# Reordered first norm, two more gate buffers, modulation transposes right behind a product, residual additions of the projection on GpSimd

## The chip, the cores and the metric

The kernel runs on one core of a Trainium2 chip. The metric is the device time of one execution in microseconds, as the median of several executions. Each engine has its own stream of instructions and works through it strictly in order; an instruction that waits for something holds up everything behind it on its engine.

## The reference, cut to what matters

The kernel computes one step of a diffusion backbone with one layer. The 128 prompt tokens and 1024 latent tokens are handled together as 9 tiles of 128 tokens, with 1024 features. Prompt and latent tokens have modulation rows of their own.

```
mod  = silu(c) @ w_mod + b_mod                       # shift1, scale1, gate1, shift2, scale2, gate2
h    = rmsnorm(x) * (1 + scale1) + shift1            # the first norm
p, v, g1, g2 = split(h @ w_in)                       # pool input, LRU input, two gates
v    = conv(v);  r, i = sigmoid(v @ w_r + b_r), sigmoid(v @ w_i + b_i)   # per head, two directions
a    = exp(-8 * r * softplus(-lambda));  u = sqrt(1 - a^2) * i * v
y    = scan(a, u) forward + scan(a, u) backward      # final prompt states are an output
m    = sigmoid(g1) * (pool(p) @ w_bp) + sigmoid(g2) * (y @ w_bl)
x    = x + gate1 * (m @ w_out)                       # "the projection"
h2   = rmsnorm(x) * (1 + scale2) + shift2            # the second norm
aff  = softmax(h2 @ router);  16 experts each take their best tokens  # expert-choice MoE
x    = x + gate2 * moe(h2);   y = rmsnorm(x)
```

## The kernel before, in words

The program's order on each engine is the order in which the code issues instructions; nothing reorders them afterwards. Weights arrive in float32 (`raw`, `araw`); a split makes of each piece a rounded high half on ACT (line L188, `hi` or `vh`) and the rest on DVE (L189, `lo` or `vl`), and a product is three products: high by high (L198), low by high (L199), high by low (L200). `do_split(n)` issues the splits up to entry n of a list, and loads run ahead of it.

**First norm (about 28 to 90 us).** The features come in eight column blocks k of 128, handled as four quarters q of two blocks. For each quarter, `mod_first` multiplies the conditioning with pieces of `w_mod` (the first four pieces in float32 at L386, the others split, L389), `mod_low` copies the sums to a small row `mrow`, `mod_second` turns that into columns on PE (L401), and DVE makes `modc` (L405) and `s` (L407) of them. `hn_first` modulates and splits block 2q in three parts (L361, L362 ACT, L365 DVE). `hn_cols` (L354 DVE, L355 ACT) and `hn_low` (L368 DVE) do it for block 2q+1. `dense_v(j, k)` multiplies block k into two accumulators, those of `v` for j = 0 and 1. `softplus` (L126 to L141) stands at the end of this stage.

**Input projection (to about 430 us).** The list `seq` orders products of w_in (`v`, `g2`, `g1`, `p`) and 256-column pieces of the modulation (`m`). Each `v` product is followed by `gates` (sigmoids, L527), `gates_rest` and `scans` of a neighbouring block. Gate tiles and the low half `yl` of a scan's result share five buffers, tag `gate`. A piece of modulation (`mod_block`, L665 and L666) leaves a row `mrow`; its transposes (`mod_cols`, L213) and their DVE part (L217, L218) are put off by five turns of the main loop, in `later`, and run at the head of a turn, ahead of its product. `pool_evac(g)` copies a `p` product to `ppad` (four ACT copies, L613 to L616), calls `pool_mm(g-1)` and then does the windowed sums that end in `ph` (L641) and `plo` (L642). `states` transposes the scans' final states, `st_c` (L692).

**Projection and routing (about 700 to 803 us).** `project(i, h)` makes tile i, half h of m @ w_out: 24 products (L984 to L986), then on DVE `tmp` = product times gate (L980) and the addition to the residual row `x2s[i]` (L981; its buffer is called `sg`, two buffers). Behind both halves come `norm2` (L992, L999, L1000, whose result is stored by SP at L1003), `router_a` (eight transposes at L1015, issued in the middle of the next tile's first half, ACT copies L1016), `router_b` (L1022) and `router_c` (L1026). The rows `x2s[i]` are loaded at L961 on SP, behind the stores of the second norm. When tiles are through, `affinities` (L1036 to L1044), `first_cols` (L1081) and `first_row` (L1092 on PE) prepare the ranks (L1111, L1114). From about 900 us on the experts run.

Of the kernel before, what the change touches and what calls it, by code (L numbers as in the profile page):

```python
# [8 lines left out]
F32 = mybir.dt.float32  # L9
# [18 lines left out]
DP = range(4)  # L28
# [21 lines left out]
def hybrid_step_kernel(ctx: ExitStack, tc: tile.TileContext, x_prompt, x_sample, state_lru, c, c_ctx,  # L50
# [70 lines left out]
    l_a = ini.tile([P, 16], F32, name="l_a")  # L121
    l_e = ini.tile([P, 16], F32, name="l_e")
    l_z = ini.tile([P, 16], F32, name="l_z")
    l_q = ini.tile([P, 16], F32, name="l_q")

    def softplus():  # L126
        A.activation(l_a, lamc, AF.Abs)
# [35 lines left out]
    s1 = const.tile([P, 2, KD], F32, name="s1")  # L163
# [131 lines left out]
    junk = xsp.tile([P, D], F32, name="junk")  # L295
    vsp = [[xsp.tile([P, 1024], F32R, name=f"v{n}{j}") for n in ("h", "l")] for j in range(2)]
# [55 lines left out]
    def hn_cols(k):  # L352
        for x, z in ((xv[:, k, 0, :SP], 0), (xv[:, k, 0, SP:], 1), (xv[:, k, 1:], 1)):
            V.tensor_scalar(x, x, s1[:, z, k:k + 1], modc[:, 0, z, k:k + 1], op0=OP.mult, op1=OP.add)  # L354
        A.copy(hn_hi[:, k, :].rearrange("p (g t) -> p g t", g=3), xv[:, k])  # L355
# [37 lines left out]
    def mod_low(q):  # L393
        mrow1[q] = xsp.tile([P, D], F32, name="mrow1", tag="junk")[:4, :512]
        A.copy(mrow1[q][:, :256], mps[q][:4, :256])
        (A.copy if q else V.tensor_copy)(mrow1[q][:, 256:], mps[q][:4, 256:])
# [32 lines left out]
    do_split(4)  # L429
    norm1(2)  # L430
    x_cols1(1, 0, A)
    x_cols1(1, 1, A)
    mod_first(0)
# [4 lines left out]
    mod_first(3)  # L438
    mod_low(0)
    do_split(5)  # L440
# [3 lines left out]
    hn_first(0)  # L444
    do_split(8)

    for q in range(4):
        k = 2 * q
        if q < 3:
            do_split(4 * q + 10)  # L450
        dense_v(0, k)
        for n in (4, 5) if q < 3 else ():
            mod_first(4 * q + n)
        hn_cols(k + 1)
        dense_v(1, k)
        for n in (6, 7) if q < 3 else ():
            mod_first(4 * q + n)
        hn_low(k + 1)
        if q < 3:
            mod_low(q + 1)  # L460
            do_split(4 * q + 12 if q < 2 else HEAD + 2)
        dense_v(0, k + 1)
        if q < 3:
            mod_second(q + 1)
        dense_v(1, k + 1)
        if q < 3:
            hn_first(k + 2)
    softplus()
# [49 lines left out]
    def gates(j):  # L518
        vc, vhi, vlo, ghi, glo = LR[j]
        gt = []  # L520
        for m in range(4):
# [4 lines left out]
            r = lt.tile([P, LT], F32, name="gate", bufs=5)  # L526
# [24 lines left out]
    def scans(j):  # L551
# [11 lines left out]
        yl = lt.tile([P, T], F32R, name="yl", tag="gate", bufs=5)  # L563
# [45 lines left out]
    def pool_evac(g, a3):  # L609
# [5 lines left out]
        for q in range(2):  # L615
            A.copy(lat[:, 4 + 6 * q:10 + 6 * q], a3[:, 1 + q, :CH].rearrange("p (r c) -> p r c", c=GW))  # L616
        if g:
            pool_mm(g - 1)
# [41 lines left out]
    def mod_block(q, h, w):  # L660
# [6 lines left out]
        if h:  # L667
            mrow = mrp.tile([4, 256], F32, name="mrow", bufs=2)
            A.copy(mrow, t[:4, :256])
            later.append([5, lambda: mod_cols(1 + q // 8, 2 * (q % 8), 2, mrow)])  # L670
# [37 lines left out]
    conv(0)  # L708
    for j in range(2):
# [12 lines left out]
    for i in range(HEAD + 2, len(seq)):  # L722
        kind, j = seq[i]
        if kind == "m" and (kind, j) not in spl and i < done_split[0]:
            continue
        if (kind, j) != ("g1", 0):
            do_split(i + 4)
        for d in list(later):
            d[0] -= 1
            if d[0] <= 0:  # L730
                d[1]()
                later.remove(d)
        if kind == "bl" and j == 0:
# [25 lines left out]
        else:  # L759
            a3 = dense(w, KD, hn_hi, hn_lo)  # L760
        if kind == "g1" and j:
# [4 lines left out]
        if kind == "v":  # L766
            v_evac(a3)
            if seq[i + 1][0] == "m":
                n = seq[i + 1][1]
                mod_block(n // 2, n % 2, spl.pop(("m", n)))  # L770
# [184 lines left out]
    def project(i, h, mid=(), part=False):  # L955
# [25 lines left out]
        V.tensor_tensor(x2s[i][:, hs], x2s[i][:, hs], tmp, op=OP.add)  # L981
# [815 lines left out]
```

## Time and profile before

| what | value |
|---|---|
| median of 3 executions | 2153.65 us (2150.96 to 2155.9) |
| the profiled execution: time, and its span in the trace | 2155.95 us, 2154.2 us |
| PE busy | 2070.4 us, 96% of the span |
| DVE busy | 1709.6 us, 79% |
| ACT busy | 1358.8 us, 63% |
| GpSimd (POOL) busy | 190.9 us, 9% |

The profiled execution is 2.3 us longer than the median; 1.75 us of its time lie outside the span. All places below are microseconds from the start of the span. A busy time in the trace is the time in which an engine executed; what its instruction waited for stands in square brackets, with the idle time before it. PEclk is the granted TensorE clock, 1.0 being 2.4 GHz and 0.5 being 1.2 GHz.

### The profile page before, as it was taken

How to read it: one execution, taken by the hardware profiler on the slowest of the kernel's cores; microseconds unless marked ns; L12 is line 12 of the kernel's file. 1: busy time of each engine (PE TensorE's matmuls, PEld its weight loads, DVE VectorE, ACT ScalarE, POOL GpSimd, SP SyncE). 2: the span in 40 equal slices, each digit the busy share in tenths (PEclk: the TensorE clock that was granted, in tenths of full speed). 3: DMA queues.
4: the chain of work that ended last, by engine and by line, in shares of the span. 5: the costliest groups of instructions: out<-in, count | busy, mean ns of one | idle time of the engine just before them, and what ended most of it. 6: DMA issues, size and time to landing. Idle time of an engine off the chain costs nothing.

```text
span 2154.2 us, 40533 instructions
## 1 busy us (share of the span) xinstructions
PE 2070.4 (96%) x17269; PEld 1974.4 (92%) x17269; DVE 1709.6 (79%) x1847; ACT 1358.8 (63%) x1444; POOL 190.9 (9%) x324
## 2 busy tenths in 40 slices
PE   6999999999999987899999999999999999999995
PEld 4799998999998875899999999999999999999994
DVE  6788988732236467988988898998998998899896
ACT  6477675321112225677877777877877777777783
POOL 0000001010101001020010010011010011011021
PEclk9999999999999988999999999999999999999997
DMA  8133434174644238699999999999999999999995
GB/s 265 56 118 114 125 111 124 55 223 117 203 158 170 109 110 296 237 326 332 346 328 334 343 331 324 343 340 326 333 335 327 338 341 328 336 341 323 339 313 181
DMA packets 304820, 543.91 MB, mean 252 GB/s; under 512 B 16300, under 2 KB 85628, under 8 KB 304639
## 3 DMA queue, kind: packets, MB, share of 16 engines
q1 hardware_dynamic: 285306, 478.56, 64.0%
q0 software_dynamic: 15728, 52.77, 8.4%
q10 hardware_dynamic: 3604, 9.98, 1.4%
q8 instruction: 135, 2.21, 0.4%
q14 instruction: 47, 0.38, 0.1%
HBM read 500.60 MB, written 40.67 MB: 251 GB/s over the span
## 4 chain that ended last, share of the span: by engine, by line
PE 86%; DVE 8%; DMA 2%; ACT 2%; issue 1%; SPq 0%; DVEq 0%; ACTq 0%
PE ac L1465 37%; PE ac L1473 17%; PE a L198 6%; PE a L199 6%; PE a L200 6%; PE a L757 5%; DVE lo L1280 2%; PE a L984 1%; PE a L986 1%; PE a L985 1%; DMA xg<-hn_d,lgi 1%; PE tp L1404 1%; PE tp L1489 1%; DVE lo L189 1%; PE tp L665 1%
## 5 line engine op out<-in xcount | busy, mean ns | idle before, releaser
L1280 DVE TENSOR_TENSOR lo<-raw,hi 128x2048 bf16<-128x2048 f32 x384 | 870.9, 2281 | 0.0
L1274 ACT CAST hi<-raw 128x2048 fp32r<-128x2048 f32 x384 | 729.4, 1912 | 3.8 <-issue 2.2
L1465 PE MATMUL ac<-x,hi 128*128 128x288 f32 x4096 | 606.1, 300 | 0.0
L1465 PEld LDWEIGHTS ac<-x,hi 128*128 128x128 f32 x4096 | 553.0, 189 | 1.0 <-issue 0.9
L1473 PEld LDWEIGHTS <-lo 128*128 128x128 bf16 x6144 | 380.4, 98 | 36.7 <-DVE lo L1280 0.8
L1465 PE MATMUL ac<-hh,hi 128*128 128x288 f32 x2048 | 332.9, 304 | 0.0
L1478 ACT COPY bs<-ac 128x288 f32<-128x288 f32 x320 | 127.8, 399 | 290.6 <-PE ac L1473 289.1
L1473 PE MATMUL ac<-xb,lo 128*128 128x144 bf16 x4096 | 302.4, 227 | 0.6 <-DVE lo L1280 0.6
L1465 PEld LDWEIGHTS ac<-hh,hi 128*128 128x128 f32 x2048 | 279.9, 189 | 0.0
L198 PE MATMUL a<-hn_hi,hi 128*128 128x384 f32 x624 | 212.0, 340 | 0.0
L199 PE MATMUL a<-hn_lo,hi 128*128 128x384 f32 x624 | 210.8, 338 | 0.0
L200 PE MATMUL a<-hn_hi,lo 128*128 128x384 f32 x624 | 210.8, 338 | 0.0
L1473 PE MATMUL ac<-hb,lo 128*128 128x144 bf16 x2048 | 171.9, 227 | 0.0
L189 DVE TENSOR_TENSOR lo<-raw,hi 128x1024 fp32r<-128x1024 f32 (+1 forms) x76 | 86.7, 1163 | 78.8 <-ACT hi L188 78.2
L1479 DVE TENSOR_TENSOR h<-ac,bs 128x288 f32<-128x288 f32 x256 | 115.7, 452 | 42.1 <-ACT bs L1478 41.8
L198 PEld LDWEIGHTS a<-hn_hi,hi 128*128 128x128 f32 x624 | 117.1, 188 | 0.4
L199 PEld LDWEIGHTS a<-hn_lo,hi 128*128 128x128 f32 x624 | 117.2, 188 | 0.0
L200 PEld LDWEIGHTS a<-hn_hi,lo 128*128 128x128 f32 x624 | 117.2, 188 | 0.0
L1710 POOL TENSOR_TENSOR yps<-ot,modc 128x128 f32<-128x128 f32 x16 | 35.9, 2247 | 735.2 <-DVE ot L1479 735.2
L188 ACT CAST hi<-raw 128x1024 fp32r<-128x1024 f32 (+1 forms) x76 | 74.8, 1001 | 41.2 <-PE a L199 33.3
L1479 DVE TENSOR_TENSOR ot<-ac,bs 128x288 f32<-128x288 f32 x64 | 29.3, 457 | 69.7 <-ACT bs L1478 69.7
L699 ACT ACTIVATE sg<-a 128x1152 f32<-128x1152 f32 x16 | 18.1, 1134 | 82.4 <-PE a L200 82.3
(447 smaller groups left out, 2626.8 us busy)
## 6 DMA issues: line engine op xcount, KB each, us to landing
raw<-in_exp_w_dram SPq DMA_DIRECT2D x380, 1024.0 KB, 7.2
raw<-in_w_in_dram SPq DMA_DIRECT2D x28, 512.0 KB, 5.0
raw<-in_w_mod_dram SPq DMA_DIRECT2D x28, 512.0 KB, 5.3
araw<-in_w_mod_dram SPq DMA_DIRECT2D x18, 256.0 KB, 4.5
g_d<-sg ACTq DMA_DIRECT2D x8, 576.0 KB, 3.2
yh_d<-yh POOLq DMA_DIRECT2D x8, 576.0 KB, 3.1
yl_d<-yl POOLq DMA_DIRECT2D x8, 576.0 KB, 4.6
m_d<-sg POOLq DMA_DIRECT2D x8, 576.0 KB, 4.2
```

Source lines behind the costliest of these rows:

```text
L188: A.copy(h, raw)
L189: V.tensor_tensor(l, raw, h.bitcast(F32), op=OP.subtract)
L198: PE.matmul(out, whi, xhi, start=first, stop=False)
L199: PE.matmul(out, whi, xlo, start=False, stop=False)
L200: PE.matmul(out, wlo, xhi, start=False, stop=last)
L757: PE.matmul(a3[:, ch, :CH], w[:, k, :], y[:, k, cs], start=n == 0 and k == 0 and w is hi, stop=n == 1 and k == KD - 1 and w is ws[-1])
L1274: A.copy(hl[n][0], raw[n])
L1280: V.tensor_tensor(lo, r, hi.bitcast(F32), op=OP.subtract)
L1465: PE.matmul(a[:, r, :2 * S], w[0][:, k, c0 + r * P:c0 + (r + 1) * P], x2(kk), start=kk == first, stop=False)
L1473: PE.matmul(a[:, r, S:2 * S], w[1][:, k, c0 + r * P:c0 + (r + 1) * P], xb(kk), start=False, stop=kk == last)
L1478: A.copy(b, a[:, :, S:2 * S])
L1479: V.tensor_tensor(dst, a[:, :, :S], b, op=OP.add)
```

## The change

There are six edits.

1. The fourth piece of modulation is split and multiplied like the later ones (`DP` is 3, not 4), and in the first norm the splits of `w_in` for the two accumulators come ahead of `mod_low(0)`. `hn_cols` is cut into `hn_mod` (DVE, now ahead of the weight splits of its quarter) and `hn_high` (ACT). `mod_low` is one ACT copy in place of two halves. The splits of the first two `g2` pieces come in the last quarter, not in the one before.
2. `softplus` runs behind `conv(0)` and takes its scratch from a gate buffer.
3. Tag `gate` has seven buffers, not five.
4. Modulation transposes have a countdown of two turns, and `turn_later` runs right behind a turn's product. `sums_next` takes the next piece of modulation right behind a `v` or `p` product; in `pool_evac` that is ahead of `pool_mm`.
5. `mrow` has one buffer.
6. The additions at L981 of tiles 1 to 7 (14 of 18) run on GpSimd; tiles 0 and 8 stay on DVE.

```diff
 FL, FM = 0, 0
-DP = range(4)
+DP = range(3)
 T = SP + SL
...
     pk = const.tile([P, 16], F32, name="pk")
-    l_a = ini.tile([P, 16], F32, name="l_a")
-    l_e = ini.tile([P, 16], F32, name="l_e")
-    l_z = ini.tile([P, 16], F32, name="l_z")
-    l_q = ini.tile([P, 16], F32, name="l_q")
     def softplus():
+        scratch = lt.tile([P, LT], F32, name="gate", bufs=7)
+        l_a, l_e, l_z, l_q = (scratch[:, 16 * n:16 * n + 16] for n in range(4))
         A.activation(l_a, lamc, AF.Abs)
...
-    def hn_cols(k):
+    def hn_mod(k):
         for x, z in ((xv[:, k, 0, :SP], 0), (xv[:, k, 0, SP:], 1), (xv[:, k, 1:], 1)):
             V.tensor_scalar(x, x, s1[:, z, k:k + 1], modc[:, 0, z, k:k + 1], op0=OP.mult, op1=OP.add)
...
+    def hn_high(k):
         A.copy(hn_hi[:, k, :].rearrange("p (g t) -> p g t", g=3), xv[:, k])
...
         mrow1[q] = xsp.tile([P, D], F32, name="mrow1", tag="junk")[:4, :512]
-        A.copy(mrow1[q][:, :256], mps[q][:4, :256])
-        (A.copy if q else V.tensor_copy)(mrow1[q][:, 256:], mps[q][:4, 256:])
+        A.copy(mrow1[q], mps[q][:4])
...
     go1(slice(6, 9))
-    do_split(4)
+    do_split(3)
     norm1(2)
...
     x_cols1(1, 1, A)
+    do_split(4)
     mod_first(0)
...
     mod_first(3)
+    do_split(6)
     mod_low(0)
-    do_split(5)
     mod_second(0)
...
     hn_first(0)
+    hn_mod(1)
     do_split(8)
...
         k = 2 * q
-        if q < 3:
-            do_split(4 * q + 10)
+        if q:
+            hn_mod(k + 1)
+        do_split(4 * q + 10 if q < 3 else HEAD + 2)
         dense_v(0, k)
...
             mod_first(4 * q + n)
-        hn_cols(k + 1)
+        hn_high(k + 1)
         dense_v(1, k)
...
         if q < 3:
+            do_split(min(4 * q + 12, HEAD))
             mod_low(q + 1)
-            do_split(4 * q + 12 if q < 2 else HEAD + 2)
         dense_v(0, k + 1)
...
             hn_first(k + 2)
-    softplus()
     do_split(HEAD + 2)
...
                 mm3(a3[:, ch, :386], ghi[:, m, :], glo[:, m, :], vhi[:, cs], vlo[:, cs], True, True)
-            r = lt.tile([P, LT], F32, name="gate", bufs=5)
+            r = lt.tile([P, LT], F32, name="gate", bufs=7)
             A.activation(r.rearrange("p (a b) -> p a b", a=3), a3[:, :, :386], AF.Sigmoid,
...
         yh = lqp.tile([P, T], F32R, name="yh", tag="lq", bufs=1)
-        yl = lt.tile([P, T], F32R, name="yl", tag="gate", bufs=5)
+        yl = lt.tile([P, T], F32R, name="yl", tag="gate", bufs=7)
         for a, b, o in ((0, SP, 0), (LL, LL + SL, SP)):
...
             A.copy(lat[:, 4 + 6 * q:10 + 6 * q], a3[:, 1 + q, :CH].rearrange("p (r c) -> p r c", c=GW))
+        sums_next(1)
         if g:
...
         if h:
-            mrow = mrp.tile([4, 256], F32, name="mrow", bufs=2)
+            mrow = mrp.tile([4, 256], F32, name="mrow", bufs=1)
             A.copy(mrow, t[:4, :256])
-            later.append([5, lambda: mod_cols(1 + q // 8, 2 * (q % 8), 2, mrow)])
+            later.append([2, lambda: mod_cols(1 + q // 8, 2 * (q % 8), 2, mrow)])
...
     conv(0)
+    softplus()
     for j in range(2):
...
             scans(0)
-    for i in range(HEAD + 2, len(seq)):
-        kind, j = seq[i]
-        if kind == "m" and (kind, j) not in spl and i < done_split[0]:
-            continue
-        if (kind, j) != ("g1", 0):
-            do_split(i + 4)
...
+    def turn_later():
         for d in list(later):
...
                 later.remove(d)
...
+    def sums_next(n):
...
+        while n and seq[at[0] + 1][0] == "m":
+            at[0] += 1
+            m = seq[at[0]][1]
+            do_split(at[0] + 1)
+            turn_later()
+            mod_block(m // 2, m % 2, spl.pop(("m", m)))
+            if m == 31 - 2 * NGT:
+                later.append([5, mod_rows])
+            n -= 1
...
+    at = [HEAD + 1]
+    while at[0] + 1 < len(seq):
+        at[0] += 1
+        i = at[0]
+        kind, j = seq[i]
+        if (kind, j) != ("g1", 0):
+            do_split(i + 4)
+        if kind == "m":
+            turn_later()
         if kind == "bl" and j == 0:
...
             a3 = dense(w, KD, hn_hi, hn_lo)
+        turn_later()
         if kind == "g1" and j:
...
             v_evac(a3)
-            if seq[i + 1][0] == "m":
-                n = seq[i + 1][1]
-                mod_block(n // 2, n % 2, spl.pop(("m", n)))
+            sums_next(1)
             gates(j - 1)
...
         V.tensor_tensor(tmp, ps, g1r[z][:, hs], op=OP.mult)
-        V.tensor_tensor(x2s[i][:, hs], x2s[i][:, hs], tmp, op=OP.add)
+        (G if 0 < i < NT - 1 else V).tensor_tensor(x2s[i][:, hs], x2s[i][:, hs], tmp, op=OP.add)
...
         PE.matmul(out, xhi, whi, start=first, stop=False)

```

In the first norm, DVE's rows from the scaling of the third tile group on, before (`vl0`, `vl1` are the low halves of `w_in` for the two accumulators, `lo` those of modulation pieces and of other weights):

```order
L309 TENSOR_SCALAR xs_136<-xs_136,rr_a_117 128x1024 x3
L342 COPY xs_136<-a3_308 128x3x4x128
L396 COPY mrow1_340<-tp_303 4x256
L189 TENSOR_TENSOR vl0_139<-raw_165,vh0_138 128x1024
L405 TENSOR_TENSOR modc_109<-tp_348,col_b_102 128x2x2x2
L407 SCALAR_TENSOR_TENSOR s1_110<-modc_109,col_a_101 128x2x2
...
L365 TENSOR_TENSOR hn_lo_129<-xs_136,hn_hi_128 128x384 x3
L189 TENSOR_TENSOR vl1_141<-raw_167,vh1_140 128x1024
L189 TENSOR_TENSOR lo_372<-araw_263,hi_371 128x1024
...
L189 TENSOR_TENSOR lo_393<-raw_345,hi_392 128x1024
L354 TENSOR_SCALAR xs_136<-xs_136,s1_110,modc_109 128x128
```

and of the change:

```order
L307 TENSOR_SCALAR xs_131<-xs_131,rr_a_112 128x1024 x3
L186 TENSOR_TENSOR lo_297<-raw_158,hi_296 128x1024
L340 COPY xs_131<-a3_308 128x3x4x128
L186 TENSOR_TENSOR vl0_135<-raw_161,vh0_134 128x1024
L186 TENSOR_TENSOR vl1_137<-raw_163,vh1_136 128x1024
L404 TENSOR_TENSOR modc_105<-tp_354,col_b_102 128x2x2x2
...
L365 TENSOR_TENSOR hn_lo_124<-xs_131,hn_hi_123 128x384 x3
L352 TENSOR_SCALAR xs_131<-xs_131,s1_133,modc_105 128x128
...
L186 TENSOR_TENSOR lo_376<-araw_259,hi_375 128x1024
```

Both `vl` rows now stand ahead of where the sums of the first quarter are there, a `lo` (the fourth modulation piece) was added ahead of them, and the modulation of block 1 (L354, now L352) went ahead of the weight splits.

On PE, the rows between the product `p` 1 and the pool product 0, before (`tp` are small result tiles, `cond` the conditioning, `ph` and `plo` the pooled sums). First the rows ahead of product `p` 1, then those behind it:

```order
L666 MATMUL tp_3109<-lo_2920,cond_169 128x256
L213 MATMUL tp_3236<-ident_82,mrow_2899 128x4 [waits DVE_49,PE_49]
L213 MATMUL tp_3236<-ident_82,mrow_2899 128x4
L198 MATMUL a3_3242<-hn_hi_128,hi_3097 128x384 [waits Activation_49]
...
L200 MATMUL a3_3242<-hn_hi_128,lo_3098 128x384
L198 MATMUL a3_3319<-ph_3210,pwh_3095 128x384 [waits DVE_49,PE_49,Activation_49]
L199 MATMUL a3_3319<-plo_3211,pwh_3095 128x384 [waits DVE_49]
...
L692 MATMUL tp_3351<-ident_82,st_c_112 16x128 [waits Activation_49]
L665 MATMUL tp_3356<-hi_3118,cond_169 128x256 [waits DVE_49,PE_49]
```

and of the change:

```order
L668 MATMUL tp_3114<-lo_2925,cond_165 128x256
L195 MATMUL a3_3241<-hn_hi_123,hi_3102 128x384 [waits PE_49,Activation_49]
L196 MATMUL a3_3241<-hn_lo_124,hi_3102 128x384
L197 MATMUL a3_3241<-hn_hi_123,lo_3103 128x384 [waits DVE_49]
...
L694 MATMUL tp_3318<-ident_82,st_c_107 16x128 [waits DVE_49,PE_49]
L210 MATMUL tp_3323<-ident_82,mrow_3214 128x4 [waits Activation_49]
L210 MATMUL tp_3323<-ident_82,mrow_3214 128x4
L667 MATMUL tp_3329<-hi_3123,cond_165 128x256 [waits Activation_49]
...
L195 MATMUL a3_3338<-ph_3225,pwh_3100 128x384 [waits DVE_49]
```

The transposes of `mrow` no longer stand ahead of product `p` 1; behind it the state transpose, `mrow` transposes and eight modulation products come ahead of the pool product instead of behind it.

In the projection, DVE's rows behind the router of tile 6, before (`sg_6413` is the residual row of tile 7):

```order
L1026 SCALAR_TENSOR_TENSOR lg_5563<-tp_6453,rr_b_120,lsh_5592 128x16
L980 TENSOR_TENSOR tmp_6463<-a2_6415,g1r1_5534 128x512
L981 TENSOR_TENSOR sg_6413<-sg_6413,tmp_6463 128x512
L1036 TENSOR_REDUCE mx_5569<-lg_5563 128x2
...
L1044 TENSOR_TENSOR lg_5563<-lg_5563,mx_5569 128x32
L1081 COPY cols_6472<-lg_5563 128x256
```

and of the change:

```order
L1046 SCALAR_TENSOR_TENSOR lg_5562<-tp_6452,rr_b_115,lsh_5591 128x16
L1000 TENSOR_TENSOR tmp_6462<-a2_6414,g1r1_5533 128x512
L1056 TENSOR_REDUCE mx_5568<-lg_5562 128x2
...
L1064 TENSOR_TENSOR lg_5562<-lg_5562,mx_5568 128x32
L1101 COPY cols_6471<-lg_5562 128x256
```

The addition is gone from DVE between `tmp` and the affinities. On GpSimd it is the last but one of 14, behind 12 of the same kind and ahead of the constants' casts:

```order
L1001 TENSOR_TENSOR sg_6283<-sg_6283,tmp_6386 128x512
L1001 TENSOR_TENSOR sg_6412<-sg_6412,tmp_6462 128x512
L1001 TENSOR_TENSOR sg_6412<-sg_6412,tmp_6519 128x512
L1143 CAST parts_5570<-lg_5562 128x96
```

Before, GpSimd had no addition there; the cast `parts` follows the last of them now.

## Rows read from the trace of the kernel before

**Rows 1.** Page, busy time by engine.
```profile
PE 2070.4 (96%) x17269; PEld 1974.4 (92%) x17269; DVE 1709.6 (79%) x1847; ACT 1358.8 (63%) x1444; POOL 190.9 (9%) x324
```

**Rows 2.** Windows: us; busy us (instructions) of PE, PEld, DVE, ACT, POOL; PEclk; DMA share; GB/s.
```profile
430.00:756.00 326.00, 326.00 (x1853) 311.11 (x1852) 127.11 (x194) 72.20 (x105) 26.81 (x139) 1.00 0.51 163
768.60:803.50 34.90, 30.75 (x129) 25.27 (x129) 18.74 (x60) 9.74 (x16) 2.28 (x5) 0.76 0.25 91
900.00:2154.00 1254.00, 1226.82 (x12272) 1187.75 (x12271) 1120.72 (x973) 951.58 (x961) 133.15 (x73) 0.99 0.94 326
```

**Rows 3.** PE's waits from 28 to 90 us: total, times, longest.
```profile
PE a L198 <- ACT hn_hi L362: 4.1, 3, 2.7
PE a L199 <- DVE hn_lo L368: 2.6, 4, 1.0
```

**Rows 4.** Timeline of PE in the first norm.
```profile
31.01 1.05 PE L401 MATMUL tp<-sum,mrow 4*128 4x2 f32 x8 [0.51 <-ACT mrow L395]
...
34.75 0.69 PE L198 MATMUL a<-hn_hi,vh 128*128 128x384 f32 x1 [2.69 <-ACT hn_hi L362]
46.31 0.45 PE L199 MATMUL a<-hn_lo,vh 128*128 128x384 f32 x1 [0.95 <-DVE hn_lo L368]
...
82.67 0.44 PE L199 MATMUL a<-hn_lo,vh 128*128 128x384 f32 x1 [0.95 <-DVE hn_lo L368]
```

**Rows 5.** Timeline of DVE in the first norm.
```profile
31.94 1.22 DVE L189 TENSOR_TENSOR vl<-raw,vh 128x1024 fp32r<-128x1024 f32 x1 [0.53 <-ACT vh L188]
33.08 0.16 DVE L405 TENSOR_TENSOR modc<-tp,col_b 128x8 f32<-128x8 f32 x1
...
37.88 3.49 DVE L189 TENSOR_TENSOR lo<-araw,hi 128x1024 fp32r<-128x1024 f32 x3
```

**Rows 6.** PE's waits from 318 to 430 us.
```profile
PE a L198 <- ACT sg L699: 2.6, 1, 2.6
PE tp L213 <- DVE modc L218: 2.1, 1, 2.1
PE a L198 <- ACT gate L527: 1.5, 1, 1.5
PE a L199 <- DVE plo L642: 0.9, 1, 0.9
```

**Rows 7.** Timeline of DVE ahead of product `p` 1.
```profile
361.24 1.22 DVE L189 TENSOR_TENSOR lo<-raw,hi 128x1024 fp32r<-128x1024 f32 x1
```

**Rows 8.** Timeline of ACT behind product `p` 1.
```profile
376.50 0.88 ACT L616 COPY ppad<-a 128x384 f32<-128x384 f32 x2
```

**Rows 9.** Timeline of all engines, tile 6's router to tile 7's addition.
```profile
769.36 1.96 PE L1022 MATMUL tp<-rws,ht 128*128 128x16 f32 x16 [0.72 <-ACT ht L1016]
...
772.45 0.68 DVE L980 TENSOR_TENSOR tmp<-a,g1r 128x512 f32<-128x512 f32 x1
772.84 0.37 SPq L961 DMA_DIRECT2D sg<-in_x_sample_dram  x1
...
776.81 0.69 DVE L981 TENSOR_TENSOR sg<-sg,tmp 128x512 f32<-128x512 f32 x1 [3.68 <-issue]
...
779.20 1.19 PE L1092 MATMUL tp<-ident,cols 128*128 128x128 f32 x4 [3.44 <-DVE cols L1081]
```

**Rows 10.** Windows of lower clock in the projection, columns as in rows 2.
```profile
771.40:774.80 3.40, 3.40 (x9) 2.65 (x9) 1.73 (x3) 0.00 (x0) 0.00 (x0) 0.50 0.47 163
778.20:791.90 13.70, 12.70 (x35) 10.18 (x36) 7.38 (x29) 2.81 (x4) 2.28 (x5) 0.50 0.10 39
```

**Rows 11.** Groups on GpSimd: busy us, mean ns of one, idle before.
```profile
L1710 POOL TENSOR_TENSOR yps<-ot,modc 128x128 f32<-128x128 f32 x16 | 35.9, 2247 | 735.2 <-DVE ot L1479 735.2
...
L1343 POOL TENSOR_TENSOR hn<-hn,t2r 128x512 f32<-128x512 f32 x2 | 2.5, 1256 | 0.2 <-ACT hn L1331 0.2
```

**Rows 12.** Timeline of DVE, one operation in two places.
```profile
769.07 0.16 DVE L156 TENSOR_TENSOR rq_b<-rq_b,rv_b 128x1 f32<-128x1 f32 x1
...
807.37 1.03 DVE L156 TENSOR_TENSOR rq_b<-rq_b,rv_b 128x1 f32<-128x1 f32 x1
```

More of the change, by code (lines that the diff above doesn't have):

```diff
@@ L162, in hybrid_step_kernel @@
     modc = const.tile([P, 3, 2, 16], F32, name="modc")
-    s1 = const.tile([P, 2, KD], F32, name="s1")
     modcol = const.tile([P, 7, KD], F32, name="modcol")
@@ L295, in hybrid_step_kernel @@
     junk = xsp.tile([P, D], F32, name="junk")
+    s1 = xsp.tile([P, 2, KD], F32, name="s1")
     vsp = [[xsp.tile([P, 1024], F32R, name=f"v{n}{j}") for n in ("h", "l")] for j in range(2)]
```

## The prediction

> **What bounds the kernel now.** I read the page's busy times first: PE executes for 96% of the span, GpSimd for 9% [rows 1]. What can be gained is PE's idle time and the time in which PE runs at the lower clock, so I went through stretches. From 430 to 756 us PE is busy for all of 326.00 us at full clock, and from 900 us on for 1226.82 of 1254 us [rows 2]; the change moves nothing into the latter, which can only start earlier. Three stretches have waits that the change touches: the first norm (28 to 90 us), the middle of the input projection (318 to 430 us) and the end of the output projection (768.6 to 803.5 us), where the granted clock was 0.76 on average [rows 2]. For each I read PE's waits and then the rows of the engine waited for.
>
> In the first norm PE waits 4.1 us for `hn_hi` and 2.6 us for `hn_lo` of L368 [rows 3]. The largest, 2.69 us, ends at 34.75 [rows 4]; the DVE row ahead of its chain is a weight split of 1.22 us at 31.94, behind which `modc` starts at 33.08 [rows 5]. In the input projection four waits matter: 2.6 (sigmoid evacuation), 2.1 (`mrow` transposes held for a small result tile), 1.5 (a sigmoid of `gates`) and 0.9 us (`plo`) [rows 6]. In the output projection DVE ends `tmp` at 773.1, then stands for 3.68 us in front of the addition L981 until 776.81 [rows 9]: the residual row's load was issued only at 772.84. Behind that addition wait the affinities and `cols`, and PE waits 3.44 us for `cols` until 779.20 [rows 9]. PE ran at half clock from 771.4 to 774.8 and from 778.2 to 791.9, busy for 3.40 and 12.70 us [rows 10]. The first of these follows a wait of 0.72 us and sixteen small router products, 1.96 us; the same products for earlier tiles lie in 430 to 756 us, with no wait ahead of them, and there the clock never fell [rows 2, 9].
>
> **A, first norm.** Both `vl` splits go ahead of the first quarter's sums, and the fourth piece of modulation is split (one DVE row more, also ahead). DVE is then free when PE's columns of `mod_second` are there (31.01 + 1.05 = 32.06 [rows 4]); with 0.2 us for the hand-over `modc` starts at about 32.3, not at 33.08: −0.8. The split's 1.22 us are not all won, since most of it ran beside those columns. The float32 products of the fourth piece become four cheaper ones; they end in front of a wait, so I count nothing. In block 1 the modulation goes ahead of four weight splits (3.49 us for three [rows 5], and a fourth of 1.22); the wait of 0.95 us at 46.31 [rows 4] goes, with small ones behind it and a weight split that no longer stands ahead of the next two `modc`: I take −3.5, of 6.7 us that rows 3 hold. Against this, two `g2` splits (2 × 1.22 us by the split in rows 5) move into the last quarter, ahead of `hn_low(7)`, whose wait, 0.95 us at 82.67 [rows 4], becomes some 2.05: +1.1, since about half of the 2.4 us falls into time in which DVE waits for ACT anyway. Sum of A: −0.8 −3.5 +1.1 = −3.2; bounds −1 (only the first gain, and nothing lost) and −5 (also a shorter stretch of lower clock). `softplus` moves off the end of this stage to a place where DVE waits for PE: 0, and 0 to +1 if it doesn't hide behind `conv(0)`.
>
> **B, input projection.** Seven gate buffers take the wait of 1.5 us away; the sigmoids no longer wait for a scan. The 2.6 us wait is that of an evacuation that sits behind ACT's own work and stays. Moving the `mrow` transposes removes the 2.1 us wait, but the third product of `p` 1 then needs a low half that DVE starts at 361.24 and has at 362.46 [rows 7], so little of it comes back at once. A new wait appears: behind `p` 1 the modulation products come ahead of the pool product, and their result tile is the one that `st_c` used, whose copy on ACT stands behind four copies to `ppad`, of which the last two take 0.88 us and start at 376.50 [rows 8]; about +1.4. At the end of the pool work PE already waits for `plo`, 0.9 us [rows 6]. That time is set by DVE's chain of windowed sums, which the change leaves as it is, so whatever PE saves ahead of it, up to 3 us, comes back there as a longer wait. The likeliest sum is 0; bounds +1 (the new wait alone) and −1.5 (the gate wait is kept).
>
> **C, projection.** Fourteen additions of 0.69 us [rows 9] leave DVE; four stay. GpSimd waits for the load in DVE's place, and DVE goes from `tmp` at 773.1 straight to the affinities. From the addition's end (777.50) to PE's start (779.20) were 1.7 us, so PE can have `cols` at about 774.8; it has done with the products ahead at 779.20 − 3.44 = 775.8, so the 3.44 us go. The same holds earlier: the ranks of the first tiles no longer sit behind an addition that waits for its load, so tile 6's chain comes earlier and most of the 0.72 us goes. Without these waits I expect PE to keep its clock: 3.40 us of work would take 1.70, and 12.70 would take 6.35, which saves 8.05. The whole is 0.72 + 3.44 + 8.05 = 12.2 us. I take 2.2 off it, for DVE rows held by a GpSimd addition and for a short stretch of lower clock that may remain: −10. Bounds: −12.2, and −5 (the two waits, 4.2, and a tenth of the rest).
>
> What an addition costs on GpSimd lies between 1.26 us (same size, L1343) and 2.25 us (L1710) [rows 11]; I take 1.26, by size and kind. It may take about 2.4 us before PE waits for it: the next tile's fifteen products until `router_a` take 15 × 0.21 = 3.2 us (3.40 us of eight steps in rows 10, halved for the full clock), less 0.68 for `tmp` and 0.1 for the hand-over. So the addition is hidden by the products; without that cover it would cost 14 × 0.57 = 7.9 us.
>
> A row tells what else it may do: DVE's L156 took 0.16 us at 769.07 but 1.03 at 807.37 [rows 12], in the middle of a GpSimd multiplication of two inputs. By this each small operation of DVE with two inputs could be held for up to one addition, 1.26 us; some six such operations follow each tile's first addition, and most have one input.
> The Trainium skill (GPSIMD Engine Reference, 1. Specifications) says that GpSimd shares its interfaces to SBUF with VectorE, with contention when DVE has two inputs in SBUF, and (4.1 Engine selection) that a two-input elementwise operation belongs on VectorE, GpSimd being about half as fast. The trace agrees: 1256 against 691 ns is 1.8 times, and the row at 807.37 fits the contention. By that rule alone, with the additions on the path, the sum of C would be +7.9 instead of −10; it is a rival below.
>
> **Sum.** −3.2 + 0 − 10 = −13.2. Against the profiled execution, 2155.95 us, this gives 2142.8; that one ran 2.3 us over the median, so on the median it is 2153.65 − 13.2 = 2140.5, rounded to 2141.
>
> **Rivals.** *GpSimd and DVE hold each other.* An addition takes 2.25 us and DVE's rank and affinity work is held by one addition in some tiles; the cols wait is partly back (up to 2 us) and a stretch of lower clock with it. For it: rows 11 and 12. Against: most DVE work there has one input. C is −6 then, and the time 2145. Chance 0.15.
> *The clock stays low.* The waits go, but small ones at the router products remain and PE falls to half clock again. For it: 0.72 us was enough at 769.36 [rows 9, 10]. C is the waits and little else, −4.5: 2146. Chance 0.12.
> *The first norm gains nothing.* The two `g2` splits hold `hn_low(7)` for their whole 2.4 us and the other waits come back at the next `modc`. A is 0: 2144. Chance 0.1.
> *Slower:* the additions on GpSimd are on the path. Each tile's `router_a` on PE waits for them; with a time t per addition, PE waits t − 2.4 us in seven tiles, which cancels 13.2 us at t = 2.4 + 13.2/7 = 4.3 us, 1.9 times the dearest row (2.25) and 3.4 times the nearest. Then the time is 2154, and with t = 5 it is 2158. Against: no GpSimd operation of this size in the trace is so slow. Chance 0.05.
> *The edits don't do what they say:* the load, not its waiter, holds `router_a(7)`. GpSimd gets the row of tile 7 at 776.8 as DVE did, but the next use of it is a tile later, so I give this 0.04; C would be −2, and the time 2148.5.
>
> **How the numbers follow.** The forecast's own case has 0.54, with 2135 to 2145 around it (A from −1 to −5, B from −1.5 to +1, C from −8 to −12.2). The rivals at 2144 to 2148.5 have 0.41 together and the slower one 0.05. The range 2134.5 to 2149.5 reaches to all but the slower and mixed cases. A measurement of this kernel tells about 0.2%, 4.3 us, from no change: faster is below 2149.3. Mixtures of two rivals (small A and small C) end at 2149 to 2152, and I put 0.1 there, with a part of the slower case; faster 0.86, same 0.1, slower 0.04.
>
> **What would show it.** Right: no PE wait over 1 us between 768 and 795 in the new times, PEclk near 1.0 there, GpSimd additions of about 1.3 us that end before `router_a` asks; the PE wait at the first big product 0.8 us shorter; no wait at a sigmoid of `gates` and a longer wait for `ph` or `plo`. Wrong: `router_a` waiting for `sg` from GpSimd, DVE rows over 1 us next to the additions, the half clock still there without a wait ahead of it, or the first norm no shorter because a weight split now stands ahead of a modulation. A gain in another stretch, above all after 900 us, would mean that a part of the sum is missing.

## The result and the profile after

The changed kernel took 2133.7 us (median of 4, 2132.4 to 2134.84) against 2152.31 for the kernel before (median of 4); the ratio is 0.9911, 95% interval 0.9894 to 0.9929, which is 15 to 23 us. It is faster, as forecast, but by 6 us more than forecast (by the ratio), and lies just below the range, which began at 2134.5. The profiled execution's span is 2131.5 us against 2154.2. Since that execution of before was a long one, the spans differ by 22.7 us and the medians by 18.6; I use the traces for places, and the medians and ratios for sizes.

The same PE instruction was looked up in both traces (start in us). The work ahead of it is the same, but for the float32 products of the fourth piece, which are now four cheaper ones, and at 306.96 two small transposes. From row to row the shift tells where the time went:

| PE instruction | before | after | shift | change of the shift |
|---|---|---|---|---|
| first big product of the first norm | 34.75 | 33.56 | −1.19 | −1.2 |
| second block of the last quarter, behind `hn_low(7)` | 82.67 | 77.88 | −4.79 | −3.6 |
| product in the input projection | 306.96 | 300.33 | −6.63 | **−1.8** |
| first product with `yp`, behind the pool part | 426.57 | 420.97 | −5.60 | +1.0 |
| router of tile 6 | 769.36 | 759.64 | −9.72 | **−4.1** |
| projection at 791.67 | 791.67 | 771.04 | −20.62 | −10.9 |
| last part | 2119.20 | 2096.81 | −22.38 | −1.8 |

The changes in bold lie where PE runs at full clock and has no wait in either trace, but for one: 0.72 of the 4.1 us are the wait at the router of tile 6 [rows 9], which is gone. No step of the prediction had a gain of the other 1.8 and 3.4 us. The last row is scatter: the kernel with 256 bytes moved (below), which gains nothing by the medians, is 2.6 us shorter in the same part of its trace.

PE's waits of the changed kernel from 28 to 90 us (total, times, longest), beside [rows 3]:

```profile
PE a L196 <- DVE hn_lo L368: 1.9, 1, 1.9
PE a L195 <- ACT hn_hi L362: 1.7, 1, 1.7
PE tp L400 <- ACT mrow L395: 1.1, 1, 1.1
PE a L196 <- DVE hn_lo L365: 0.5, 3, 0.2
```

The four waits for `hn_lo` of `hn_low` (L368) have become one, that of `hn_low(7)`, and it is twice as long (0.95 before, 1.9 now). The wait for `hn_hi` is 1.7 instead of 4.1 in all. From 318 to 430 us, beside [rows 6]:

```profile
PE a L195 <- ACT sg L701: 3.2, 1, 3.2
PE a L197 <- DVE lo L186: 1.6, 1, 1.6
PE a L195 <- DVE ph L643: 1.6, 1, 1.6
PE tp L667 <- ACT mr L696: 1.2, 1, 1.2
PE a L196 <- DVE plo L644: 0.9, 1, 0.9
```

The gate wait and the transposes' wait are gone; a low half (L186), the copy of the states' tile (`mr`) and a longer wait for `ph` stand in their place. Behind the last of them PE ran at half clock for 3.4 us, which the trace of before does not have there (window as in [rows 2]):

```profile
418.00:421.40 3.40, 3.40 (x16) 3.40 (x15) 0.90 (x1) 1.86 (x2) 0.00 (x0) 0.50 0.67 198
```

The end of the projection, timeline of the engines behind tile 6's router, beside [rows 9]:

```profile
761.92 0.68 DVE L1000 TENSOR_TENSOR tmp<-a,g1r 128x512 f32<-128x512 f32 x1
762.31 0.37 SPq L981 DMA_DIRECT2D sg<-in_x_sample_dram  x1
762.51 0.18 DVE L1056 TENSOR_REDUCE mx<-lg 128x2 f32<-128x32 f32 x1
...
763.86 0.29 DVE L1101 COPY cols<-lg 128x256 f32<-128x256 f32 x1
764.30 0.57 PE L1112 MATMUL tp<-ident,cols 128*128 128x128 f32 x3
```

The load is issued right behind `tmp` as before, but DVE no longer stands in front of it: from `tmp` to the first affinity there is no gap, and PE's use of `cols` carries no wait. The group of the additions, and two windows (us, busy us of PE, PEld, DVE, ACT, POOL with instructions, PEclk, DMA share, GB/s):

```profile
L1001 POOL TENSOR_TENSOR sg<-sg,tmp 128x512 f32<-128x512 f32 x14 | 18.0, 1290 | 84.3 <-DMA sg<-in_x_sample_dram 38.9 <-DVE tmp L1000 33.6 <-PE a L1006 11.8
```

```profile
769.00:785.00 16.00, 14.86 (x82) 12.44 (x80) 11.75 (x38) 7.79 (x12) 3.52 (x6) 1.00 0.45 156
786.70:796.90 10.20, 9.52 (x27) 3.95 (x27) 7.46 (x26) 4.74 (x7) 5.85 (x9) 0.50 1.01 357
```

An addition takes 1.29 us, near the 1.26 taken [rows 11]. The clock is full where [rows 10] had the half; from 786.7 us, behind the projection, comes a stretch of half clock of 10 us, where before there was one of 7 us from 808.9. So the sign "PEclk near 1.0" between 768 and 795 us held only up to 786.7.

Another sign, one of being wrong, did come: a DVE row over 1 us next to an addition. L1134, an operation of the ranks with two inputs, took 0.35 us in six of its eight rows there, as it did before (L1114, 0.35 in all six), but 1.24 beside the addition that starts at 750.57:

```profile
749.46 0.35 DVE L1134 SCALAR_TENSOR_TENSOR beat<-arow,lg,tri 128x128 bf16<-128x128 f32 x1
...
750.57 1.30 POOL L1001 TENSOR_TENSOR sg<-sg,tmp 128x512 f32<-128x512 f32 x1 [9.78 <-DMA sg<-in_x_sample_dram]
...
750.78 1.24 DVE L1134 SCALAR_TENSOR_TENSOR beat<-arow,lg,tri 128x128 bf16<-128x128 f32 x1
```

It ends 0.15 us behind the addition. PE waits for nothing there, so this cost PE nothing.

### The profile page after: what moved, and what is told of

Same layout as the page of the kernel before. It is cut to its first block, busy times and chain, and to the rows that moved or that the text cites. A ratio compares the mean times of both kernels' runs of the same rounds, so it can differ in the third digit from the quotient of the medians.

```text
span 2131.5 us, 40527 instructions
## 1 busy us (share of the span) xinstructions
PE 2056.4 (96%) x17269; PEld 1962.2 (92%) x17269; DVE 1703.2 (80%) x1833; ACT 1359.8 (64%) x1442; POOL 208.9 (10%) x338
## 4 chain that ended last, share of the span: by engine, by line
PE 88%; DVE 7%; ACT 2%; DMA 2%; issue 1%; SPq 0%; DVEq 0%; ACTq 0%; POOLq 0%
PE ac L1485 37%; PE ac L1493 17%; PE a L196 6%; PE a L197 6%; PE a L195 6%; PE a L778 5%; DVE lo L1300 2%; PE a L1004 2%; PE a L1006 2%; PE a L1005 2%; DMA xg<-hn_d,lgi 1%; PE tp L1042 1%; PE tp L667 1%; PE tp L1424 1%; PE tp L1509 1%
## 5 line engine op out<-in xcount | busy, mean ns | idle before, releaser
L186 DVE TENSOR_TENSOR lo<-raw,hi 128x1024 fp32r<-128x1024 f32 (+1 forms) x77 | 88.3, 1165 | 64.4 <-ACT hi L185 64.4
L1335 POOL DMA_INDIRECT xg<-hn_d,lgi x16 | 45.0, 2813 | 258.4 <-ACT bs L1498 138.2
```

What stands on the lines that cost most here:

```text
L186: V.tensor_tensor(l, raw, h.bitcast(F32), op=OP.subtract)
```

## Experiments

Each was timed in several rounds beside the kernel before; the ratio is to that kernel.

### Where do 4 us without a wait come from?

In the stretches in bold, PE's products of 384 columns follow each other more closely. In each, 128×128 weights (`hi` or `lo`) meet a moving operand of 384 columns (`hn`, `y` or `yp`). In the products with `y` (line L757, or L778 in the changed kernel) nothing else is in the way; here are the starts of the second and of the seventh of eight blocks of 72 products, timeline of PE, before and after:

```profile
577.94 0.34 PE L757 MATMUL a<-y_hi,hi 128*128 128x384 f32 x1
641.39 0.34 PE L757 MATMUL a<-y_hi,hi 128*128 128x384 f32 x1
```

```profile
570.50 0.34 PE L778 MATMUL a<-y_hi,hi 128*128 128x384 f32 x1
633.01 0.34 PE L778 MATMUL a<-y_hi,hi 128*128 128x384 f32 x1
```

That is 63.45 and 62.51 us for 360 products: 176.2 and 173.6 ns each, the pitch. Some 2700 products of this kind (1872 with `hn`, 576 with `y`, 288 with `yp`) × 2.6 ns are 7 us at most. One part of the change, which neither the list of edits nor the lines of the diff above show, touches them without being on any path: `s1`, 64 bytes, moved out of the constants into another pool, and with it everything behind it in SBUF lies 64 bytes lower, the moving operands `hn`, `yp` and `y` among them, while the weights' buffers `hi` and `lo` stay. By the built program's addresses, the distance from moving operand to weights is 128 modulo 256 before and 192 after (all slices of both lie whole multiples of 256 bytes apart, so one number holds for all products). Three theories: the distance counts, the moving operand's own offset counts, or the new order of instructions does it.

**s1 moved alone.** The kernel before with

```diff
-    s1 = const.tile([P, 2, KD], F32, name="s1")
...
+    s1 = xsp.tile([P, 2, KD], F32, name="s1")
```

> The kernel before, with the 64-byte tile s1 taken out of the constants and put behind junk, as in the change; nothing else. All operands of the input products (hn_hi, hn_lo, y, yp) move down by 64 bytes, from 96 to 32 above a multiple of 128; the weights' buffers (hi, lo) stay at 96. In the change the same products follow each other at about 173.5 ns, before at about 176, which over some 2700 products of 384 columns is 6 to 7 us. Address theory in both forms (the moving operand's own offset counts, or its offset relative to the weights'): pitch 173.5 and 6 to 7 us less than before. Order theory (the pitch came from the reordered transposes and splits): pitch 176 and no change.

**Weights moved alone.** The kernel before with 64 bytes ahead of the weights' pool:

```diff
+    padr = ctx.enter_context(tc.tile_pool(name="padr", bufs=1, side="right"))
+    pad_r = padr.tile([P, 16], F32, name="pad_r")
     wp = wstk.enter_context(tc.tile_pool(name="wp", bufs=4, side="right"))
```

> The kernel before, with 64 bytes reserved above the weights' buffers, so that hi and lo move from 96 to 32 above a multiple of 128; hn_hi, hn_lo and the others stay at 96. Relative form of the address theory (equal offsets of the two operands cost 2.5 ns a product): pitch 173.5, 6 to 7 us less. Own-offset form (the moving operand at 96 is slow wherever the weights are): pitch 176, no change. Order theory: no change.

**Both moved**, the two edits together.

> The kernel before with both moves: s1 out of the constants and 64 bytes above the weights, so that moving operands and weights all stand at 32 above a multiple of 128. Relative form: equal offsets again, pitch 176, no change. Own-offset form: pitch 173.5, 6 to 7 us less. Order theory: no change.

**The changed kernel with another 64 bytes moved:**

```diff
-        q = const.tile([P, n], F32, name=f"rq_{tag}")
+        q = (ini if tag == "a" else const).tile([P, n], F32, name=f"rq_{tag}")
```

> The changed kernel with another 64-byte tile (rq_a) taken out of the constants, so that hn and the others stand at 96 above a multiple of 128 again, as in the kernel before, and the weights at 96. Both forms of the address theory: pitch back at 176, 6 to 7 us more than the changed kernel, so about 0.994 of the kernel before. Order theory: pitch 173.5 and the changed kernel's time, 0.991 of before.

The first gave 0.9979 (0.9966 to 0.9991), the second 0.9981 (0.9973 to 0.999), the third 0.9998 (0.9989 to 1.0007): one move is worth 4 us, both together nothing. So it is the distance, not either operand's own place, and not the order. The 6 to 7 us expected of a move did not come by the medians; they lie within the interval of the first (2 to 7 us) but not of the second (2 to 6), in which a part of the products kept the long pitch (last section). The two rows for `s1` moved alone, and for both moved:

```profile
573.49 0.34 PE L757 MATMUL a<-y_hi,hi 128*128 128x384 f32 x1
636.00 0.34 PE L757 MATMUL a<-y_hi,hi 128*128 128x384 f32 x1
```

```profile
580.52 0.34 PE L759 MATMUL a<-y_hi,hi 128*128 128x384 f32 x1
643.99 0.34 PE L759 MATMUL a<-y_hi,hi 128*128 128x384 f32 x1
```

62.51 and 63.47 us for the 360 products. The fourth missed what both address forms expected: its offsets are equal modulo 128 again, and yet it kept the short pitch and the changed kernel's time (0.9916, 0.9903 to 0.9929). Either the rule goes by 256 bytes (its distance is 0 modulo 256, not 128), or the new order has a part in it after all. Three more kernels, all in the old order, told these apart.

**128 bytes moved** (`s1`, and `rq_a` as above), **256 bytes moved** (`rv_a` and `rr_a` as well), and **32 bytes added** to the constants:

```diff
+    pad_c = const.tile([P, 8], F32, name="pad_c")
     modcol = const.tile([P, 7, KD], F32, name="modcol")
```

> The kernel before with 128 bytes taken out of the constants (s1 and rq_a), nothing else. The weights' buffers then stand at 0 from the moving operands modulo 256 (128 in the kernel before, 192 and 64 in the two quick experiments). If only the distance 128 of 256 is slow: pitch 173.5 and 4 us less. If equal offsets modulo 128 are slow, as the first three experiments alone would say: pitch 176, no change, and the last experiment of that call was quick for another reason, one that lies in the changed kernel's order.

> The kernel before with 256 bytes taken out of the constants (s1 and the three small tiles of the first norm), so that all distances are those of the kernel before plus 256. If the rule repeats every 256 bytes: pitch 176 and no change. If it repeats every 512 or more: pitch 173.5 and 4 us less.

> The kernel before with 32 bytes more of constants, so that the distance is 96 modulo 256 and the moving operands start on a multiple of 128. If only distances near 128 are slow, this one (32 away from it) tells how near: pitch between 173.5 and 176. An own-offset effect of a start on a multiple of 128 would show as a pitch under 173.

The rows for 128 and for 256 bytes moved:

```profile
574.23 0.34 PE L757 MATMUL a<-y_hi,hi 128*128 128x384 f32 x1
636.75 0.34 PE L757 MATMUL a<-y_hi,hi 128*128 128x384 f32 x1
```

```profile
579.50 0.34 PE L757 MATMUL a<-y_hi,hi 128*128 128x384 f32 x1
642.97 0.34 PE L757 MATMUL a<-y_hi,hi 128*128 128x384 f32 x1
```

| kernel | distance mod 256 | 360 products, us | ratio to before (interval) |
|---|---|---|---|
| before | 128 | 63.45 | 1 |
| both moved | 128 | 63.47 | 0.9998 (0.9989 to 1.0007) |
| 256 bytes moved | 128 | 63.47 | 0.9994 (0.9983 to 1.0005) |
| s1 moved | 192 | 62.51 | 0.9979 (0.9966 to 0.9991) |
| weights moved | 64 | 62.52 | 0.9981 (0.9973 to 0.999) |
| 32 bytes added | 96 | 62.51 | 0.998 (0.9966 to 0.9993) |
| 128 bytes moved | 0 | 62.52 | 0.9971 (0.996 to 0.9982) |
| changed | 192 | 62.51 | 0.9911 (0.9894 to 0.9929) |
| changed, 64 more bytes moved | 0 | 62.52 | 0.9916 (0.9903 to 0.9929) |

In all nine kernels the products with `y` have the long pitch when the distance is 128 modulo 256, and at none of 0, 64, 96 and 192. The order of the instructions has no part in it. The four quick kernels in the old order have a mean ratio of 0.9978: 4.8 us (4.3 by the medians). The changed kernel with the distance back at 128 was not run: the one that was meant to be that had 0.

### The parts of the sum, one at a time

**The additions alone**, in the kernel before, and **the additions back on DVE**, in the changed kernel: the line of edit 6, the other way round in the second.

> The kernel before with the 14 additions of the projection on GpSimd and nothing else. The two traces show 10.9 us of the gain between 768 and 792 us of the old times. Cover theory (GpSimd waits for the load in DVE's place, no PE wait over 1 us is left there and the clock stays full): 10 to 11 us less than before, ratio about 0.995. Shared-interface theory (DVE is held beside the additions and part of the gain in the changed kernel came from the earlier stages): about 6 us less, and DVE rows over 1 us beside the additions.

> The changed kernel with all additions on DVE again. Cover theory: the waits for the load and for cols are back with the stretches of half clock, 10 to 11 us more than the changed kernel, 0.996 of the kernel before. If the earlier stages alone had moved the waits away: the changed kernel's time, 0.991.

Measured: 0.9955 (0.9942 to 0.9968), 9.7 us less than before, and 0.996 (0.9947 to 0.9973), 9.4 us more than the changed kernel. The cover theory holds from both sides; a DVE row of 1.24 us beside an addition came in the first too (L1114 at 759.46), without the loss that the other theory put on it. The additions' kernel has PE busy throughout at full clock where [rows 10] lie; the other one has the wait for `cols` back, and two stretches of half clock, but these last 6.9 us together and not the 17.1 of [rows 10]. One window of the first, one wait and two windows of the second:

```profile
766.00:785.00 19.00, 19.00 (x109) 16.00 (x107) 14.46 (x53) 8.44 (x15) 4.80 (x7) 1.00 0.29 111
```

```profile
PE tp L1112 <- DVE cols L1101: 3.4, 1, 3.4
```

```profile
763.90:767.40 3.50, 3.50 (x10) 2.58 (x8) 1.16 (x3) 0.00 (x0) 0.00 (x0) 0.51 0.65 228
770.80:774.20 3.40, 3.09 (x9) 2.67 (x10) 1.55 (x7) 0.37 (x1) 2.19 (x5) 0.50 0.01 2
```

**The first norm alone**, with `s1` moved (edit 1 of the change, and the 64 bytes).

> The kernel before with s1 moved (as in the first experiment, about -4.4 us by itself) and the new order of the first norm alone (the fourth piece split, splits, modulation and weight splits in the new order, one copy for the row of sums). The two traces show 4.8 us at the end of that stage. If these are the reorder's own: about 9 us less than before, 0.9957; if the stage's gain is lost later: the first experiment's time, 0.998.

0.9959 (0.9943 to 0.9976). Against `s1` alone (0.9979) this is 4.3 us for the reorder, with intervals of about ±3 us on each ratio; between the two traces it is 5.3 us at 83 us. Its wait at `hn_low(7)` is the changed kernel's:

```profile
PE a L198 <- DVE hn_lo L370: 1.9, 1, 1.9
```

**Gates and transposes alone**, with `s1` moved (edits 2 to 5).

> The kernel before with s1 moved (-4.4 us by itself), seven gate buffers, softplus behind conv(0), and the modulation transposes and sums right behind the products; first norm and additions as before. My term for this was 0, and the traces show +1.1 us. Give-back theory (the gate wait and the transposes' wait go, and PE waits as long for the pooled sums and for the copy of the states' tile): 3 to 4.5 us less than before, 0.998 to 0.9985, with a wait for ph or plo longer than before. Rival: the waits removed are worth their 3.6 us, and the time is 8 us less, 0.9963.

0.998 (0.997 to 0.999), the same as `s1` alone: the four edits together are worth nothing that can be told from noise (about 3 us), as the give-back theory has it, and the rival's 0.9963 is excluded. Its waits are the changed kernel's, the first three of five:

```profile
PE a L195 <- ACT sg L697: 3.2, 1, 3.2
PE a L197 <- DVE lo L186: 1.7, 1, 1.7
PE a L195 <- DVE ph L639: 1.6, 1, 1.6
```

### Inside the two reordered stages

**Pool product first**, in the changed kernel:

```diff
-        sums_next(1)
         if g:
             pool_mm(g - 1)
+        sums_next(1)
```

> The changed kernel with the pool product ahead of the modulation sums again in the pool part, and all else as changed. Give-back theory: the pool products run about 1 us earlier, so DVE's chain from pool product 2 to ph and plo of group 3 ends about 1 us earlier and the wait there shrinks from 2.5 to 1.5 us; the wait of 1.2 us for the states' tile is hidden by the pool product. 1 to 3 us less than the changed kernel (3 with the stretch of half clock at 418 gone). Rival: DVE's chain hangs on the scans, not on the pool product; the time stays.

**The g2 splits early**, in the changed kernel, and then **both**:

```diff
-            do_split(min(4 * q + 12, HEAD))
+            do_split(4 * q + 12 if q < 2 else HEAD + 2)
```

> The changed kernel with the two g2 splits in the third quarter of the first norm again, as before the change. My term for their move was +1.1 us, at the wait for hn_low(7), which is 1.9 us in the changed kernel: that wait is 0.9 us then, and 1 us less in all, unless the splits hold modc of the fourth quarter instead, with a longer wait for hn_hi and no gain.

> The changed kernel with both of the edits before: if each is worth what its theory says, 2 to 4 us less than the changed kernel, ratio 0.989 to 0.990 of the kernel before.

**Five gate buffers**, in the changed kernel (`bufs=5` at tag `gate`).

> The changed kernel with five gate buffers. The wait for a gate buffer, 1.5 us at 328.8 in the kernel before, comes back. Give-back theory (DVE's chain sets when the pool products end, so what PE saves ahead of it is lost there): the changed kernel's time within 1 us. Rival (the two buffers are worth their wait): 1.5 to 3 us more.

They gave 0.9915 (0.9899 to 0.9931), 0.9909 (0.9892 to 0.9925), 0.9908 (0.9892 to 0.9925) and 0.992 (0.9905 to 0.9934). None can be told from the changed kernel's 0.9911; the lowest median, 2132.17 us for both edits, is 1.5 us below it (0.6 by the ratios), so the 2 to 4 us expected of both are not shown. The traces say more. With the pool product first, the wait for `ph` falls from 1.6 to 0.4 us, but that for the states' tile grows from 1.2 to 2.3: my expectation that the pool product hides it was wrong. PE is 0.3 us behind the changed kernel at 317 us and 0.6 at 418, so the waits gave nothing; at 422 it is 0.9 ahead, where the half clock from 418.0 is missing. With the g2 splits early, the wait at `hn_low(7)` is 1.0 instead of 1.9:

```profile
PE a L196 <- DVE hn_lo L368: 1.0, 1, 1.0
```

With five gate buffers the gate wait comes back, larger:

```profile
323.01 0.45 PE L195 MATMUL a<-vhi,ghi 128*128 128x386 f32 x1 [2.55 <-ACT gate L528]
```

PE is 0.8 us behind the changed kernel ahead of that wait (its trace has a stretch of half clock at 78 us that the other has not) and 3.7 us behind it. The later waits, for the low half, the states' tile, `ph` and `plo`, are as long as in the changed kernel to 0.1 us, so DVE's chain gives nothing back, against the give-back theory. From 422 to 759 us PE is 2.2 us behind, since the half clock from 418.0 is not there, and from 797 us on within about 1 us, as the stretches of half clock behind the projection fall differently (10.2 us from 786.7 in the changed kernel, 6.8 us from 788.1 in this one). So the place speaks for the rival; the measured time (1.9 us more by the ratios, 0.8 by the medians) decides nothing.

## Why the prediction was right or wrong

**What bounds the kernel: the step that failed.** The prediction said "What can be gained is PE's idle time and the time in which PE runs at the lower clock", and took the 326.00 busy us of [rows 2] as fixed. They were not: PE was busy there at full clock, and its 384-column products still followed each other 1.5% further apart than they need, by where two buffers lie. That is 4.8 us by the four kernels that did nothing else, the largest part of the 6 us by which the forecast missed. The trace of before hardly shows this, since all its products with `hn`, `y` and `yp` have the long pitch; the whole diff has a tile that moves to another pool, and I asked of the edits only which waits change, not what lies elsewhere afterwards.

**A, first norm: mechanism right, gain perhaps too small.** Forecast −3.2, measured −4.3 alone (−4.8 in the trace); the 1.1 us between them are within the noise of the two ratios. The first product gained 1.2 instead of 0.8 us, as `modc` started at 31.88 and not at the 32.3 taken; the middle, until the first product of block 6 (77.27 before, 71.52 now), 4.6 instead of 3.5; the term for the g2 splits was +1.1, and the trace shows +1.0, which the kernel with early splits took back at that wait.

**B, input projection: sum right, in part by luck.** Forecast 0, measured 0, to about 3 us. The low half of `p` 1 (1.6 us), the states' tile (1.2 against the 1.4 taken) and the longer wait for `ph` all came as written. But I put the whole give-back on DVE's chain of sums, as a time that the change leaves as it is. The kernel with five gates shows that a delay ahead of the chain moves all that follows, and the one with the pool product first that the tile of the states holds PE whichever product stands ahead of it. A part of what the removed waits gave went into the half clock from 418.0 us, which the kernel with these edits alone also has (422.1 to 425.5) and the one with `s1` alone has not; the prediction had no term for it.

**C, projection: mechanism right, size in part by luck.** Forecast −10, measured −9.7 alone. The load, the wait for it, `cols`, the two waits of PE and the two stretches of half clock went as written, and an addition took 1.29 us. But the 8.05 us for the clock were read from one execution, in which the two stretches lasted 17.1 us together. In nine other kernels with all additions on DVE the half clock there lasted 6.8 to 17.1 us, behind the same wait for `cols` (3.4 to 5.0 us). From 768 to 791.67 us the additions alone gained 11.8 us in the trace, nearly the whole 12.2; that the medians show 9.7 fits the profiled execution of before, which ran 3.6 us over the median of 2152.3. The 2.2 us were taken off for another reason, held DVE rows and a remaining stretch, and neither cost anything here.

The rival of shared interfaces was right about the row and wrong about its price: L1134 was held for 0.9 us beside one addition, under the bound of 1.26 in the prediction, in work that PE was not waiting for. DVE's affinity rows shown above tell nothing on it, because no addition ran beside them: the additions around them ran from 755.35 to 756.64 and from 766.36. The Trainium skill (GPSIMD Engine Reference, 1. Specifications) has contention for DVE operations with two SBUF inputs; L1134 agrees, and so does L156 (L154 in the changed kernel), 1.03 us beside a GpSimd multiplication behind the projection. The Trainium skill's rule on the choice of engine (GPSIMD Engine Reference, 4.1 Engine selection) would have kept the additions on DVE; here the 1.9 times longer addition is hidden, and what counts is which engine stands in front of the load.

**Sum.** −4.8 (distance) − 4.3 − 0 − 9.7 = −18.8, against −19.2 from the ratio. The parts add up, closer than they are known (each to 2 to 4 us); the forecast's −13.2 lacked the first term, and perhaps 1 us of the second.

## What to carry to other kernels

When a saturated engine gets faster without a wait going, compare the pitch of equal instructions in a stretch without waits, and look at which addresses moved: any tile added, resized or moved to another pool shifts all behind it. An engine that queues behind a late load costs what stands behind it in its queue; giving that one wait to an idle engine was worth ten microseconds, though the operation itself became nearly twice as long. A removed wait in a stage with several chains is worth what the next one leaves: measure such edits alone before believing them. Price a stretch of half clock from more than one execution.

## What the runs showed of the hardware

- Products of 128×128 weights with 384 columns at full clock follow each other at 173.6 ns, but at 176.3 when moving operand and weights lie 128 bytes apart modulo 256; at distances of 0, 64, 96 and 192 the products with `y` are quick, and others were not tried. In the weights-moved kernel (64) those with `hn` come close (median 174 ns), yet those with `yp` kept a median of 176; so distance 64 is not quick for every buffer, and why is open. What in the chip does it was not tried.
- How long PE stays at half clock behind a wait differs between kernels with the same instructions in that place. In the ten traces with all additions on DVE, around a wait of 3.4 to 5.0 us for `cols`, PE was at half clock for 6.8 or 6.9 us in five, for 10.3 in one, and for 13.6 to 17.1 in four; the same work of PE, from 779.20 to 791.67 us before, took 4.3 us less in the kernel with 128 bytes moved.
- A DVE operation with two inputs, begun 0.2 us into a GpSimd addition, ended only 0.15 us behind it: L1134 took 1.24 us at 750.78, against 0.35 without an addition beside it.
